# Two layers of a diffusion backbone on one core: one feed-forward input product by Strassen's scheme, and the adaLN modulations on TensorE

## The chip, the core and the metric

The kernel runs on one core of one Trainium2 chip, in one launch. The metric is the device time of that core in microseconds. Five engines run side by side, each through its own list of instructions, in the order in which they stand there: TensorE (PE in the profile; its weight loads are PEld), VectorE (DVE), ScalarE (ACT), GpSimd (POOL) and SyncE (SP), which here issues most DMAs. They wait for each other with semaphores.

## The reference

512 latent tokens and 256 context tokens of 1024 numbers, all float32. Each of two layers is a half-step SwiGLU feed-forward network (FFN), a mixer of four head groups, and a second FFN. Cut to what the change touches:

```
ml = ada_mods(silu(c), w_ada[l], b_ada[l])      # 9 * 1024 numbers for the latent tokens,
mc = ada_mods(silu(c_ctx), w_ada[l], b_ada[l])  # and as many for the context tokens
y = modulate(rms_norm(h, g), shift, scale)
a, b = split(y @ w_i, 2, axis=-1)               # w_i [1024, 5632]
h = h + 0.5 * gate * ((silu(a) * b) @ w_o)      # w_o [2816, 1024]
```

FFN 1 and FFN 2 of layer 0 and FFN 1 of layer 1 are needed for all 768 tokens, FFN 2 of layer 1 for the 512 latent ones alone.

## The kernel before

Everything lies transposed: features on the 128 partitions, tokens along the row. The residual is eight tiles `h[j]` of [128, 768]. `hg_tile` makes the input of a product from each (the residual times gain and scale, the shift in two columns ahead of the tokens, so that a product has 770 columns), split in two float32r parts, high and low. The RMS factor `R` of a token is multiplied in behind the product.

`wload` brings 1 MB of weights (8 row blocks, 256 columns) to a `wraw` buffer of three; `wsplit` makes the high part `wh` on ACT (L378) and the low part `wl` on DVE (L379), of 128 columns at a time, in two buffers each. `mm` (L389) then multiplies three times for each row block: high by low, low by high, high by high. A product of 770 columns goes to two PSUM banks, as 258 columns and 512, so a column tile of 1024 rows takes 48 matmuls on PE.

`ffn` walks over 22 column tiles `f` of the hidden layer. Each takes two products (`a` and `b`, 96 matmuls), is multiplied by `R`, gets silu and product on ACT and DVE (L448 to L455), and is split into `uh` and `ul` (L458 ACT, L459 POOL). After each group of `FF` = 5, 5, 4, 4, 4 tiles the output product of that group follows: eight tiles `po`, each added to `h[j]` by DVE (L495).

The modulations are 18 pieces of 512 columns a layer. The first four of layer 0 are multiplied on TensorE by `ada_first` (L215): float32, two columns of weights, written to PSUM partitions 0, 32, 64 and 96 in turn. The other 32 pieces are made by `ada_steps`, as `hooks` between the column tiles: 16 multiply-adds of [128, 512] on DVE (L254, L256), then four float32 matmuls by ones, to the four strips of 32 PSUM partitions (L263), a copy on ACT (L265) and two transposes on PE (L268).

What is written in the code is not the order on the engines: a scheduler reorders the list of each engine when the program is built, so matmuls of several products stand mixed. The engines then run those fixed lists.

The mixer (`Mixer.run`) multiplies 16 column tiles by `w_in`, with S5 and RG-LRU work between them, then attention, then `out_proj` (L1236), whose last steps call `hg_tile` for the next FFN. `park` and `unpark` keep the residual in DRAM meanwhile.

## Time and profile before

| | us |
|---|---|
| median of 3 runs | 2879.5 (2876.4 to 2881.92) |
| the profiled execution, first to last instruction | 2877.7 |

| stage of the profiled execution | us | PE busy | DVE busy |
|---|---|---|---|
| start, to 81.6 | 81.6 | 65.5 | 54.6 |
| rest of layer 0 FFN 1, to 655.7 | 574.1 | 568.3 | 405.5 |
| layer 0 mixer, to 1021.4 | 365.7 | 352.7 | 237.3 |
| layer 0 FFN 2, to 1595.8 | 574.4 | 574.1 | 308.3 |
| layer 1 FFN 1, to 2180.5 | 584.7 | 584.2 | 352.2 |
| layer 1 mixer, to 2484.7 | 304.2 | 289.1 | 207.4 |
| layer 1 FFN 2 and final norm, to the end | 393.0 | 385.2 | 177.0 |

The page gives for each engine its busy time and, for groups of instructions, how often they ran, their time together and the mean of one. Matmuls are pipelined: a row's mean is longer than the step from one matmul to the next, so steps are read from a run of many, or from starts. A float32 matmul stands in the trace as two records (34 matmuls at L357 are 68 records), a float32r one as one.

### The profile page before, as it was taken

To read this page: it belongs to the slowest core of one execution; us is meant where nothing else is said; L and a number is where in the kernel's file an instruction comes from. 1 tells how busy PE (TensorE), PEld (TensorE's weight loads), DVE (VectorE), ACT (ScalarE), POOL (GpSimd) and SP (SyncE) were. 2 spreads that over 40 slices of the span, in tenths; PEclk is the share of its full clock that TensorE was granted. 3 is DMA by queue.
4 is the path that set the end of the run, shared out by engine and by line. 5 is a ranking of instruction groups with operands and counts; after the bars stand their busy time and mean duration, and the time that the engine had idled before them with its cause. 6 is when DMAs were issued, how large, how long until landed. Compare 5 with 4: busy or idle time off the path is not lost.

```text
span 2877.7 us, 43478 instructions
## 1 busy us (share of the span) xinstructions
PE 2819.1 (98%) x17293; PEld 2437.7 (85%) x17293; DVE 1742.3 (61%) x3178; ACT 906.5 (32%) x1478; POOL 757.7 (26%) x957
## 2 busy tenths in 40 slices
PE   7999999999999999999999999999999999999998
PEld 4888888888877888888888888888888887899998
DVE  6868577676857566363634766465466876444445
ACT  4212121235546422112123321222224645322223
POOL 2822233221323311000001176332312434201001
PEclk9999999999999999999999999999999999999999
DMA  6445324353323333222311335233254343232231
GB/s 227 134 108 167 112 96 141 123 185 118 115 62 74 103 115 99 87 96 95 107 54 54 118 101 142 80 123 106 74 168 145 118 106 89 79 96 83 88 96 52
DMA packets 295901, 312.13 MB, mean 108 GB/s; under 512 B 58991, under 2 KB 243202, under 8 KB 295698
## 3 DMA queue, kind: packets, MB, share of 16 engines
q1 hardware_dynamic: 266990, 293.97, 31.8%
q0 software_dynamic: 5664, 12.59, 1.9%
q10 hardware_dynamic: 23044, 2.78, 0.7%
q8 instruction: 137, 2.24, 0.3%
q14 instruction: 66, 0.54, 0.1%
HBM read 276.09 MB, written 29.02 MB: 106 GB/s over the span
## 4 chain that ended last, share of the span: by engine, by line
PE 88%; DVE 6%; DMA 2%; ACT 2%; issue 1%; POOL 0%; SPq 0%; ACTq 0%; DVEq 0%; POOLq 0%
PE pi L389 51%; PE po L389 23%; PE po L1236 4%; DVE acc L256 2%; PE po L862 2%; PE pt L810 2%; DMA wa<-in_w_ada_dram 1%; PE ps L793 1%; PE pa L263 1%; DVE wl L379 1%; PE ps L794 1%; DMA l<-in_w_ada_dram 1%; PE pl L734 1%; DVE z L455 0%; PE pa L215 0%
## 5 line engine op out<-in xcount | busy, mean ns | idle before, releaser
L389 PE MATMUL pi<-g,wh 128*128 128x258 f32 (+2 forms) x6656 | 1408.7, 330 | 8.4 <-ACT wh L378 2.6
L389 PEld LDWEIGHTS pi<-g,wh 128*128 128x128 f32 x6656 | 1101.4, 191 | 132.2 <-issue 15.0
L389 PE MATMUL pi<-g,wl 128*128 128x258 f32 (+2 forms) x3328 | 828.1, 329 | 0.7 <-DVE wl L379 0.7
L378 ACT CAST wh<-wr 128x1024 fp32r<-128x1024 f32 (+3 forms) x380 | 338.2, 890 | 1397.4 <-PE pi L389 674.8
L389 PEld LDWEIGHTS pi<-g,wl 128*128 128x128 f32 x3328 | 607.4, 191 | 60.6 <-issue 2.5
L389 PE MATMUL po<-l,wh 128*128 128x512 f32 (+1 forms) x2464 | 566.1, 344 | 0.9 <-DVE e L495 0.8
L389 PEld LDWEIGHTS po<-l,wh 128*128 128x128 f32 x2464 | 387.9, 188 | 63.9 <-issue 3.9
L459 POOL TENSOR_TENSOR l<-z,l 128x768 fp32r<-128x768 f32 (+1 forms) x88 | 159.1, 1808 | 1061.4 <-ACT l L458 955.4
L379 DVE TENSOR_TENSOR wl<-wr,wh 128x1024 fp32r<-128x1024 f32 (+3 forms) x380 | 407.0, 1071 | 50.3 <-ACT wh L378 47.5
L256 DVE SCALAR_TENSOR_TENSOR acc<-wa,s,acc 128x512 f32<-128x512 f32 x448 | 358.6, 849 | 39.4 <-DMA wa<-in_w_ada_dram 38.6
L495 DVE SCALAR_TENSOR_TENSOR e<-po,gt,e 128x512 f32<-128x512 f32 (+1 forms) x296 | 176.2, 631 | 307.4 <-PE po L389 250.7
L389 PE MATMUL po<-l,wl 128*128 128x512 f32 (+1 forms) x1232 | 337.5, 343 | 1.0 <-DVE wl L379 1.0
L453 DVE TENSOR_TENSOR z<-pi,R 128x768 f32<-128x768 f32 (+2 forms) x91 | 78.4, 865 | 301.3 <-PE pi L389 301.3
L389 PEld LDWEIGHTS po<-l,wl 128*128 128x128 f32 x1232 | 194.5, 188 | 32.6 <-DVE wl L379 2.0
L448 DVE COPY bc<-pi 128x2 f32<-128x2 f32 x88 | 13.7, 156 | 189.4 <-PE pi L389 189.4
L458 ACT CAST l<-z 128x768 fp32r<-128x768 f32 (+1 forms) x88 | 68.8, 782 | 160.5 <-DVE z L455 160.5
L1545 POOL TENSOR_TENSOR ww<-AR,BB 128x256 f32<-128x256 f32 x32 | 25.9, 808 | 341.4 <-PE pw L1564 309.5
L455 DVE SCALAR_TENSOR_TENSOR z<-z,pi,z 128x512 f32<-128x512 f32 (+1 forms) x154 | 107.1, 730 | 5.5 <-ACT z L451 0.7
L317 POOL TENSOR_TENSOR ssq<-ssq,sq 128x768 f32<-128x768 f32 (+1 forms) x35 | 67.5, 1929 | 161.0 <-ACT sq L316 161.0
L451 ACT ACTIVATE z<-z,bc 128x512 f32<-128x512 f32 (+1 forms) x154 | 90.0, 625 | 62.7 <-DVE z L449 51.3
L449 DVE TENSOR_TENSOR z<-pi,R 128x768 f32<-128x768 f32 (+1 forms) x88 | 77.5, 880 | 3.7 <-ACT R L366 3.7
L1236 PE MATMUL po<-l,wh 128*128 128x512 f32 (+1 forms) x264 | 71.9, 356 | 0.0
(349 smaller groups left out, 2632.0 us busy)
## 6 DMA issues: line engine op xcount, KB each, us to landing
wr<-in_w_ffn_in_dram SPq DMA_DIRECT2D x88, 1024.0 KB
wa<-in_w_ada_dram SPq DMA_DIRECT2D x64, 1024.0 KB
wr<-in_w_ffn_out_dram SPq DMA_DIRECT2D x48, 512.0 KB
wr<-in_w_ffn_out_dram SPq DMA_DIRECT2D x32, 640.0 KB
wr<-in_w_in_dram SPq DMA_DIRECT2D x16, 1024.0 KB
W<-s5w SPq DMA_DIRECT2D x32, 256.0 KB
wr<-in_w_out_dram SPq DMA_DIRECT2D x8, 1024.0 KB
l<-in_w_ada_dram SPq DMA_DIRECT2D x24, 256.0 KB
```

The costliest lines, as they stand in the source:

```text
L256: nc.vector.scalar_tensor_tensor(acc[r], raw[:, k], s, acc[r], ALU.mult, ALU.add)
L378: nc.scalar.copy(hi[:, :kn], raw[:, :, o:o + P])
L379: nc.vector.tensor_sub(lo[:, :kn], raw[:, :, o:o + P], hi[:, :kn].bitcast(F32))
L389: nc.tensor.matmul(dst, lhsT=wt[:, k, :], rhs=xt[:, a:b], start=(k == 0 and i == 0), stop=(k == kn - 1 and i == 2))
L449: nc.vector.tensor_mul(ta[:, :nt], pa[:, 256:256 + nt], self.R[:, :nt])
L451: nc.scalar.activation(ta[:, a:b], ta[:, a:b], AF.Silu, bias=bc[:, i:i + 1])
L453: nc.vector.tensor_mul(tb[:, a:b], p, self.R[:, a:b])
L455: nc.vector.scalar_tensor_tensor(tb[:, a:b], tb[:, a:b], pb[:, 254 + i:255 + i], ta[:, a:b], ALU.add, ALU.mult)
L458: nc.scalar.copy(uh[:, :nt], tb[:, :nt])
L459: nc.gpsimd.tensor_sub(ul[:, :nt], tb[:, :nt], uh[:, :nt].bitcast(F32))
L495: self.nc.vector.scalar_tensor_tensor(self.h[j][:, a:b], ps[:, a:b], gate[:, j, i:i + 1], self.h[j][:, a:b], ALU.mult, ALU.add)
L1236: self.nc.tensor.matmul(dst, lhsT=wt[:, k, :], rhs=xt[:, a:b], start=(c == 0 and i == 0), stop=(c == NT - 1 and i == 2))
```

## The change

1. `STRASSEN` names layer 0's FFN 2. There the 2 by 2 blocks are: `a` and `b` columns of the weights, even and odd row blocks of 128, first and second 384 tokens. `st_tile` makes seven input combinations, each split in two parts, during `out_proj`. `st_weights` makes seven weight combinations from raw weights, four of them on POOL, and `two` splits them. `st_in` runs seven products of 4 row blocks and 384 or 386 columns (12 matmuls each), each to a PSUM tile of its own, and DVE adds them up in SBUF; the multiplication by `R` goes to POOL.
2. `ada_steps` multiplies on TensorE: eight float32 matmuls of 512 columns with 32 columns of weights, to the strips of 32 PSUM partitions in turn, and four small float32 matmuls by `sel` in place of the transposes. DVE keeps the bias alone.
3. Products of 770 columns are cut 386 and 384 instead of 258 and 512.
4. `wload` brings 128 columns (0.5 MB) of an input product at a time; `wraw` has five buffers of half the size.
5. `FF` is 4, 4, 4, 4, 3, 3. Tiles and pools move: the cosines and sines are loaded in the mixer to two `z` tiles, the low parts for `out_proj` lie in `g` and `e` tiles.

```diff
-SLOTS = {"e": 8, "l": 12, "z": 5, "g": 16}
+SLOTS = {"e": 8, "l": 12, "g": 16}
+Z_SLOTS, X_SLOTS = 5, 12
+W_BUFS = {"wh": 2, "wl": 2, "ws": 1}
-FF = (5, 5, 4, 4, 4)
+FF = (4, 4, 4, 4, 3, 3)
-        self.wraw = ent(tc.tile_pool(name="wraw", bufs=3))
+        self.wraw = ent(tc.tile_pool(name="wraw", bufs=5))
...
     def ada_steps(self, l, q):
...
         def rows(k0):
-            raw = (ring() if ring else self.wraw).tile([P, 4, 512], F32, name=self.nm("wa"), tag="wraw")
-            for k in range(4):
-                for r in range(2):
-                    s = self.s2[:, k0 + k, r:r + 1]
...
-                        nc.vector.scalar_tensor_tensor(acc[r], raw[:, k], s, acc[r], ALU.mult, ALU.add)
+            if k0 == 0:
+                st["ps"] = self.bank("pa", "pst")
+            for k in range(k0, k0 + 4):
+                if k % 2 == 0:
+                    raw = self.wraw.tile([P, 2, 512], F32, name=self.nm("wa"), tag="wraw")
+                    nc.sync.dma_start(raw, ...)
+                o = 32 * (k % 4)
+                nc.tensor.matmul(st["ps"][o:o + 32], lhsT=self.s2w[:, 2 * k:2 * k + 32], rhs=raw[:, k % 2], start=(k < 4), stop=(k >= 4))
         def done():
-            for i in range(4):
-                nc.tensor.matmul(ps[32 * i:32 * i + 32], lhsT=self.ones.to_broadcast([P, 32]), rhs=acc[i // 2]..., start=True, stop=True)
-            nc.scalar.copy(arow, ps)
-            for b in range(2):
-                nc.tensor.transpose(pt[:, b * P:(b + 1) * P], arow[:, b * P:(b + 1) * P], self.ident)
+            nc.scalar.copy(arow, st["ps"])
+            for b in range(4):
+                nc.tensor.matmul(pt[:, 2 * b:2 * b + 2], lhsT=arow[:, b * P:(b + 1) * P], rhs=self.sel, start=True, stop=True)
...
     def in_chunks(self, ps, nt):
-        return (ps[:, 254:512], (0, 258)), (ps[:, 512:256 + nt], (258, nt + 2))
+        o, m = self.at(nt), nt // 2 + 2
+        return (ps[:, o - 2:512], (0, m)), (ps[:, 512:o + nt], (m, nt + 2))
...
+    def st_weights(self, ra, rb):
+        (a11, a12), (a21, a22) = ((t[:, :4], t[:, 4:]) for t in (ra, rb))
+        s12 = self.wtile("ws", F32)
+        s2, s1 = s12[:, :4], s12[:, 4:]
+        yield from parts(ra)
+        G.tensor_add(s1, a21, a22)
+        G.tensor_sub(s2, s1, a11)
+        yield from parts(s12)
+        G.tensor_sub(a11, a11, a21)
+        G.tensor_sub(a12, a12, s2)
+        yield from parts(ra)
+        yield from parts(a22)
+    def st_in(self, ra, rb, nt):
+        def product(i, n):
+            dst = self.bank("pi") if i % 2 else self.psb.tile([P, 1024], F32, name=self.nm("pi"), tag="psb")
+            self.mm(((dst[:, :n], (0, n)),), next(ws), lambda k: self.sx[k][i], 4)
+            return dst[:, :n]
+        nc.scalar.copy(c21, product(0, w))
+        V.tensor_add(c11, product(1, w), c21)
+        V.tensor_add(c21, product(2, w), c21)
+        V.tensor_add(c12, product(3, m), c21[:, :m])
+        p = product(4, w)
+        V.tensor_add(c21, p, c21)
+        V.tensor_add(c22, p[:, :m], c12)
+        V.tensor_add(c12, product(5, m), c12)
+        nc.gpsimd.tensor_mul(a_, a_, R)
...
+        V.tensor_add(c21, product(6, w), c21)
+        nc.gpsimd.tensor_mul(b_, b_, R)
...
+STRASSEN = ((0, "ffn2"),)
```

How it moves instructions, at two places of layer 0's FFN 2. On PE before, a piece of modulation was one run of matmuls between two output tiles (`pa` is the PSUM strip, `po` an output tile, x2 two in a row to different strips):

```order
L389 MATMUL po_12341<-l_12186,wh_12337 128x512
L389 MATMUL po_12341<-l_12186,wh_12337 128x256
L263 MATMUL pa_12857<-acc_12713,ones 32x256 x2
L263 MATMUL pa_12857<-acc_12715,ones 32x256 x2
L389 MATMUL po_12372<-l_11486,wh_12368 128x512
L389 MATMUL po_12372<-l_11486,wh_12368 128x256
```

On PE of the changed kernel, in the second column tile of that FFN, between two of the seven products (L424 is `mm`, L282 a modulation product, L291 the small ones by `sel`):

```order
L424 MATMUL pi_10148<-x_9736,wh_10151 128x386
L424 MATMUL pi_10148<-x_9736,wl_10152 128x386
L424 MATMUL pi_10148<-x_9736,wh_10151 128x386
L282 MATMUL pa_10245<-wa_10396,s2w 32x512 x2
L291 MATMUL pt_10101<-sel,l_10099 128x2 x4
L424 MATMUL pi_10134<-g_9252,wh_10117 128x386
L424 MATMUL pi_10134<-g_9252,wl_10118 128x386
```

The eight products of a piece stand in several such runs, mostly of two. In the whole program the 256 products stand in 93 runs: 57 of two, 12 of one, 4 of three, 10 of four, 10 of six or eight; the 128 matmuls by ones stood in 44 runs.

On ACT before, in the same FFN, a column tile needs two weight parts (L378), and they stand among silu (L451) and the split (L458):

```order
L378 CAST wh_11092<-wr_11088 128x1024
L451 ACTIVATE z_11063<-z_11063,bc_11062 128x512
L451 ACTIVATE z_11063<-z_11063,bc_11062 128x256
L378 CAST wh_11145<-wr_11090 128x1024
L458 CAST l_11072<-z_11064 128x768
L378 CAST wh_11233<-wr_11088 128x1024
```

On ACT of the changed kernel (L410 is the weight part, `ws` sums made on POOL, L614 the first of the seven PSUM tiles, L288 a modulation's copy):

```order
L410 CAST wh_10117<-wr_10107 128x1024
L625 ACTIVATE l_9950<-l_9950 128x512
L625 ACTIVATE l_9950<-l_9950 128x256
L410 CAST wh_10151<-ws_10116 128x1024
L535 CAST l_10078<-l_9951 128x768
L288 COPY l_10099<-pa_10082 128x512
L614 COPY l_10114<-pi_10115 128x386
L410 CAST wh_10185<-wr_10107 128x1024
L410 CAST wh_10221<-wr_10110 128x512
L410 CAST wh_10264<-wr_10254 128x1024
```

A column tile now takes three and a half parts of this size from the same two buffers, and the fourth, `wh_10221`, serves the last product alone.

## Rows read from the trace of the kernel before

**Rows 1.** The page: span, engines' busy time, and the granted clock in 40 slices.
```profile
span 2877.7 us, 43478 instructions
PE 2819.1 (98%) x17293; PEld 2437.7 (85%) x17293; DVE 1742.3 (61%) x3178; ACT 906.5 (32%) x1478; POOL 757.7 (26%) x957
PEclk9999999999999999999999999999999999999999
```
**Rows 2.** Stretches of FFNs: length, busy us (instructions) by engine, granted clock, DMA.
```profile
81.60:480.00 398.40, 396.80 (x2293) 340.30 (x2293) 279.65 (x450) 85.29 (x126) 154.04 (x217) 1.00 0.39 120
480.00:520.00 40.00, 36.43 (x198) 29.34 (x197) 35.52 (x46) 8.41 (x16) 16.22 (x16) 0.91 0.51 172
520.00:655.70 135.70, 135.02 (x777) 115.18 (x776) 90.37 (x147) 41.66 (x76) 34.26 (x29) 1.00 0.50 161
1021.40:1595.80 574.40, 574.12 (x3284) 495.87 (x3284) 308.28 (x489) 135.93 (x194) 53.55 (x31) 1.00 0.28 90
1595.80:2180.50 584.70, 584.21 (x3390) 506.75 (x3389) 352.17 (x619) 143.24 (x227) 222.64 (x338) 1.00 0.38 118
```
**Rows 3.** Chain that ended last: start, length, what; runs of one kind of matmul.
```profile
1325.59 34.10 PE pi L389 x192
...
2555.91 27.82 PE po L389 x120
2583.73 57.89 PE pi L389 x480
```
**Rows 4.** Timeline of PE: start, length, count; a run of L215, two float32 products.
```profile
44.60 0.39 PE L389 MATMUL pi<-g,wh 128*128 128x512 f32 x1
44.92 1.03 PE L215 MATMUL pa<-l,s 128*2 128x512 f32 x4
45.88 0.50 PE L389 MATMUL pi<-g,wh 128*128 128x512 f32 x1
46.22 0.40 PE L389 MATMUL pi<-g,wl 128*128 128x512 f32 x1
```
**Rows 5.** Timeline of PE: ten float32 products in one run.
```profile
53.09 1.46 PE L215 MATMUL pa<-l,s 128*2 128x512 f32 x10
53.97 0.59 PE L215 MATMUL pa<-z,s 128*2 128x512 f32 x2
54.38 0.60 PE L215 MATMUL pa<-l,s 128*2 128x512 f32 x2
54.40 1.44 PE L215 MATMUL pa<-z,s 128*2 128x512 f32 x6
```
**Rows 6.** Timeline of PE: a run of L263, two float32 products of 256 columns.
```profile
1171.69 0.51 PE L389 MATMUL pi<-g,wh 128*128 128x258 f32 x2
1172.13 0.62 PE L263 MATMUL pa<-acc,ones 128*32 128x256 f32 x4
1172.69 0.62 PE L389 MATMUL pi<-g,wl 128*128 128x258 f32 x2
1173.14 0.63 PE L389 MATMUL pi<-g,wh 128*128 128x258 f32 x3
```
**Rows 7.** Groups by shape: count, busy us, mean ns, idle before and releaser.
```profile
L268 PE MATMUL pt<-ident,z 128*128 128x128 f32 x64 | 12.2, 272 | 0.0
L357 PE MATMUL pr<-ones,ssq 128*128 128x1 f32 x68 | 8.5, 251 | 0.0
L378 ACT CAST wh<-wr 128x1024 fp32r<-128x1024 f32 x224 | 235.3, 1050 | 896.9 <-PE pi L389 518.7 <-issue 187.8 <-PE po L389 115.1
L379 DVE TENSOR_TENSOR wl<-wr,wh 128x1024 fp32r<-128x1024 f32 x224 | 285.9, 1276 | 30.3 <-ACT wh L378 28.1
L459 POOL TENSOR_TENSOR l<-z,l 128x768 fp32r<-128x768 f32 x66 | 127.2, 1927 | 736.5 <-ACT l L458 672.4 <-issue 47.1 <-DMA wa<-in_w_ada_dram 16.9
L951 POOL TENSOR_TENSOR e<-e,cos 128x512 f32<-128x512 f32 x6 | 9.8, 1648 | 10.0 <-PE pr L948 10.0
```
**Rows 8.** Who PE waited for: total us, times, longest.
```profile
PE pa L263 <- DVE acc L256: 4.2, 4, 2.1
```

More of the change, by code (lines that the diff above doesn't have):

```diff
@@ L72, in setup @@
         self.cols = [c.tile([P, P], F32, name=f"cols{l}") for l in range(3)]
-        self.cos, self.sin = (c.tile([P, TL], F32, name=x) for x in ("cos", "sin"))
         self.perm = c.tile([P, P], F32, name="perm")
@@ L155, in load_vectors @@
         if l == 2:
-            self.s2 = self.const.tile([P, NT, 2], F32, name="s2")
+            self.s2w = self.const.tile([P, 2 * NT + 30], F32, name="s2w")
+            nc.vector.memset(self.s2w, 0.0)
+            self.s2 = self.s2w[:, :2 * NT].rearrange("p (k r) -> p k r", r=2)
             for i in range(2):
                 nc.scalar.activation(self.s2[:, :, i], self.cols[2][:, 8 * i:8 * i + 8], AF.Silu)
+            self.sel = self.const.tile([P, 2], F32, name="sel")
+            strips = self.ident.rearrange("p (g x) -> p g x", g=4)[:, :, 0:2]
+            nc.vector.tensor_add(self.sel, strips[:, 0], strips[:, 1])
+            for g in (2, 3):
+                nc.vector.tensor_add(self.sel, self.sel, strips[:, g])
     def col(self, l, name, i=0, n=1):
@@ L388, in mm @@
                 for dst, (a, b) in chunks:
-                    nc.tensor.matmul(dst, lhsT=wt[:, k, :], rhs=xt[:, a:b], start=(k == 0 and i == 0),
+                    nc.tensor.matmul(dst, lhsT=wt[k], rhs=xt[:, a:b], start=(k == 0 and i == 0),
                                      stop=(k == kn - 1 and i == 2))
@@ new lines, in st_weights, with parts @@
+    def st_weights(self, ra, rb):
+        G = self.nc.gpsimd
+        (a11, a12), (a21, a22) = ((t[:, :4], t[:, 4:]) for t in (ra, rb))
+        def parts(w):
+            hi, lo = self.two(w)
+            for i in range(0, len(hi), 4):
+                yield hi[i:i + 4], lo[i:i + 4]
+        s12 = self.wtile("ws", F32)
[8 more added lines that the diff above has]
+        yield from parts(a22)
@@ L945, in gqa_turn @@
         n, nc = self.n, self.nc
+        cos, sin = (self.t("z", w=TL) for _ in range(2))
+        nc.sync.dma_start(cos, self.A["k_cos"])
+        nc.sync.dma_start(sin, self.A["k_sin"])
         for src in self.gts:
@@ L1235, in out_proj @@
                     for dst, (a, b) in ch:
-                        self.nc.tensor.matmul(dst, lhsT=wt[:, k, :], rhs=xt[:, a:b], start=(c == 0 and i == 0),
+                        self.nc.tensor.matmul(dst, lhsT=wt[k], rhs=xt[:, a:b], start=(c == 0 and i == 0),
                                               stop=(c == NT - 1 and i == 2))
@@ L1632, in body @@
         hooks = [[] for _ in range(NFF)]
-        ring = []
         if not last:
-            spread(hooks, [s for q in range(ADA_2) for s in n.ada_steps(1, q, lambda: ring[0])])
+            spread(hooks, [s for q in range(ADA_2) for s in n.ada_steps(1, q)])
         end = None if last else lambda j: fin(j, 1, "ffn1", "g_ffn1", 0, TT)
-        with tc.tile_pool(name=n.nm("ring"), bufs=3 if last else 2, reuse_waits="tile") as more:
-            ring.append(more)
-            n.ffn(l, A["w_ffn2_in"][l], A["w_ffn2_out"][l], lambda: n.gate(l, 8, 0.5), nt, end, hooks, ring=more if last else None)
+        n.ffn(l, A["w_ffn2_in"][l], A["w_ffn2_out"][l], lambda: n.gate(l, 8, 0.5), nt, end, hooks)
+        n.room(0 if last else Z_SLOTS, 0)
         if not last:
```

234 lines of the change are left out of this document (155 added, 79 removed).

## The prediction

> **What bounds the kernel now.** I read the page first. PE is busy for 2819.1 of 2877.7 us [rows 1], but that alone says little, since matmuls overlap; so I looked next at the stretches of the FFNs [rows 2]. In layer 0's FFN 2 PE is busy for 574.12 of 574.40 us, in layer 1's FFN 1 for 584.21 of 584.70, at full clock. In the third, from 81.6 to 655.7, PE idles for 1.6 + 3.6 + 0.7 = 5.9 us, and only between 480 and 520 is the granted clock below full (0.91). Whether "busy" means "at its pace" is seen from runs in the chain [rows 3]: 192 matmuls of two column tiles took 34.10 us, a step of 0.1776 us; 480 of 256 or 258 columns took 57.89 us, 0.1206 each; 120 of 512 columns took 27.82 us, 0.2318 each. The two column tiles in the middle of a layer, with all its side work, run at the pace that the two sizes give together (0.1206 + 0.2318 = 0.352 a pair, against 0.355). So in the FFNs PE's list is the time. DVE is not behind it: PE waited for the modulations' sums on DVE for 4.2 us in all [rows 8], in 4 waits. From this I take the method: count what the change takes from PE's list and what it puts in, price both from rows, and then ask where PE would newly wait.
>
> **Strassen's products.** A column tile had 96 matmuls of 385 columns on average; seven products of 12 are 84. 22 tiles x 12 = 264 matmuls less, at 0.1776 us: **-46.9 us**, all of it on the path, as PE had no idle time there [rows 2, 3].
>
> **The modulations on TensorE.** Added are 256 float32 products of 512 columns, in 93 runs. Their price is read from the first modulations, which have that size and go to strips of 32 partitions [rows 4]. From 44.60 to 46.22 there are 1.62 us, in which two float32r matmuls of 512 columns would have taken 2 x 0.2318; so a run of two products (four records) costs 1.15 us. Where ten stand together [rows 5], a new set of records begins 0.43 us after the last one (53.97, 54.40); a product has two passes, so a round is 0.86 us, and up to four products to different strips share one. The remaining 0.29 us is the way in and out. That the number in a round doesn't matter is also seen from the old matmuls by ones [rows 6]: from 1171.69 to 1173.14 are 1.45 us, less four float32r matmuls (two of the pairs above, 0.71) is 0.74 for two products of 256 columns, and 0.74 is again one round of half the length (0.43) plus 0.31. So what counts is the number of runs and rounds, and not that of the products. 83 runs have one round and 10 have two (six or eight products over four strips): 83 x 1.15 + 10 x 2.01 = 115.6 us.
>
> The Trainium skill's page "TensorEngine Tiling (Array Packing)", section Overview / Key Properties, says that a change of the tiling mode drains the engine. The trace agrees: 0.3 us beyond the rounds at each run.
>
> Added too are 128 small products by `sel`, 256 records; nearest is L357, 8.5 us for 68 records [rows 7], 0.125 each: 32 us. Removed are 44 runs of matmuls by ones at 0.74 = 32.6 us, and 64 transposes, 12.2 us [rows 7]. Together 115.6 + 32 - 32.6 - 12.2 = **+102.8 us** on PE. Bounds: 103 rounds at 0.86 with nothing lost on the way in and out would be 27 us less; if the small products cost what a transpose does (0.19), 17 us more.
>
> **DVE is relieved** of 16 operations a piece. What PE can get from it is what PE lost to it: the 3.6 us of idle time between 480 and 520, and 40 x 0.09 = 3.6 us of slow clock there [rows 2]: **-7 us** (0 to -10, with the other 2.3 us of idle time in that FFN).
>
> **A new short distance on the weights' buffers.** Two `wh` and two `wl` buffers remain. Before, a buffer served 48 matmuls, 8.5 us, and the next split had that long. Now it serves two products, 24 matmuls or 4.26 us, and the one for the seventh product 12 matmuls, 2.13 us. The split for the next tile's first two products can start only when the fifth and sixth are done, and only the seventh covers it. ACT needs 1.05 us and DVE 1.28 behind it [rows 7], 2.33 us before any queueing, against 2.13. Since ACT and DVE run in order and have sums, silu and splits queued, I take 0.5 us a tile: 22 x 0.5 = **+11 us**. It can be nothing, where runs of modulations or output tiles stand between, and 2 us a tile (44) at worst, when a sum and a silu always stand ahead. POOL has four sums of 512 (1.65 each by L951), two multiplications of 768 (1.93 by L459, which is a subtraction) and one subtraction of 768 a tile: 12.4 us of the 14.9 that seven products take; it fits, with little to spare, and before the output tiles it has time to recover.
>
> **The start of that FFN.** The last residual tile `h[7]` gets its place in SBUF from the low part of `out_proj`'s last operand, so its load from DRAM starts only when `out_proj` ends, and then come the residual's addition, scaling, splits and the sum of squares. PE has the first three row block pairs of four products to go on with, 36 matmuls or 6.4 us. I take **+3 us** (0 to 8), and **+2 us** (0 to 10) for both mixers, where the same holds and two of five `z` tiles now hold cosines and sines while S5 uses the others.
>
> **The even cut.** 386 and 384 columns in place of 258 and 512 give the same number of matmuls and columns. If the step is proportional to columns it costs nothing: 0.2318 / 512 = 0.453 ns a column against 0.1206 / 257 = 0.469 for the short one. No row has 384 columns, so the bounds are these two: 770 columns at 0.453 is 0.349 a pair and at 0.469 is 0.361, against 0.355, so -6 to +6 ns; with some 5,400 pairs (24 a product tile of 768 tokens, 24 a row block of outputs, so 1584 an FFN in three FFNs, some 130 fewer with Strassen, and 800 in the mixers) that is -33 to +33 us. I take **0**, as the mean of the two is the step of the mixed run. The groups of `FF` change no count on PE, smaller loads are off the path (DMA share 0.28 to 0.39 in the long stretches [rows 2]), and the start is bound by the first modulations, which stay: 0.
>
> **The sum.** -46.9 + 102.8 - 7 + 11 + 3 + 2 = +64.9. From the profiled execution's 2877.7 that is 2942.6; it lay 1.8 us below the median of the runs, so I forecast **2944 us**, slower by 2.2%. The saved matmuls are worth less than half of what the modulations add to the one engine that had no room, while DVE, which did them beside, had.
>
> **The rivals.**
>
> *Products packed four at a time.* 256 products over four strips are 64 rounds at least, 55 us in place of 115.6 if the way in and out were free: 2944 - 61 = 2883, no change. It would need PE to fill strips across the matmuls that stand between; its list is fixed, 69 of the 93 runs hold one or two products, and the runs of the old kernel paid for each stop [rows 6]. Chance 0.05.
>
> The Trainium skill's "TensorEngine Tiling (Array Packing)", Overview / Theoretical Speedup, gives up to four times for products of 32 columns or less; by that rule the rounds would be those 64. No row here shows strips shared across other matmuls.
>
> *The strips run beside the main stream.* A modulation product uses a quarter or a half of the array's columns. If the matmuls around it went on meanwhile, the 115.6 us would vanish: 2944 - 116 = 2828, faster by 1.8%. The place is each of the 93 runs, the price 0 to 1.15 us, and it turns the sign where a run costs less than about 0.45 us. Against it: between 44.92 and 45.88 no float32r matmul started [rows 4], nor between 1172.13 and 1172.69 [rows 6]. Chance 0.05.
>
> *The weights' split becomes the bound of Strassen's stage.* At 2 us a tile PE stands for 44 us rather than 11: 2977; with POOL late as well (12.4 of 14.9 us), another 1 us a tile: 3000. For it: three chained engines and 0.2 us too little cover before any queue. Against: ACT and DVE have time (ACT's stage total was 136 of 574 us, DVE's 308 with the modulations in it [rows 2]). Chance 0.13.
>
> *Strassen's saving doesn't come*, since a product of half the depth pays for its start: nothing in the steps shows a price for a new PSUM tile. It would be 2991. Chance 0.03.
>
> **How the numbers follow.** The forecast, with the even cut at either bound, has 0.73 (2905 to 2985); the others as given, 0.01 left. Slower by over 0.2% (about what a measurement of this kernel can tell from no change): 0.73 + 0.13 + 0.03 = 0.89; same: 0.05; faster: 0.06. The range takes in the low bound of the products and of the even cut (together, -40 rather than their sum of -60, as they are independent) and on the other side the split's bound: 2904 to 2990.
>
> **What would show it.** In the profile after, L282 should have 512 records, and PE's main stream a gap of 1.1 to 1.2 us at each of its runs, also where two products stand alone. The seven products should run at 0.177 us a matmul, so that layer 0's FFN 2 has 22 x 14.9 + 187 us of L424, and with nine pieces of modulation (3.2 each) ends some 4 us below its 574. Layer 1's FFN 1 should be longer by about 9 x 3.2 = 29 us and layer 0's by more, though DVE is nearly free there. A wait of PE for `wl` once in a tile shows the buffers. I am wrong at the root if the FFNs without Strassen don't grow, wrong in size if the L282 gaps are not 1.15 us, and if the output tiles change their step from 0.355 a pair, it is the even cut.

## The result, and the profile after

The changed kernel takes **3021.4 us** (median of 4 runs, 3019.0 to 3022.7) against 2878.3 (4 runs) before: a ratio of **1.0498, 95% interval 1.0483 to 1.0513**. Slower was right; 5.0% instead of the 2.2% forecast was not, and 3021 lies 31 us outside the range of 2904 to 2990. The profiled execution has 3020.2 us against 2877.7, so +142.5 us are to be explained where +64.9 were forecast.

First the page of the changed kernel: PE has 89.6 us more busy time than in [rows 1], so 53 us of the 142.5 are PE standing still.

```profile
span 3020.2 us, 44606 instructions
PE 2908.7 (96%) x17453; PEld 2673.8 (89%) x17453; DVE 1553.1 (51%) x2897; ACT 974.4 (32%) x1602; POOL 919.6 (30%) x1117
```

Then the changed kernel by stretches: FFN 1 of layer 0, its mixer, its FFN 2 (Strassen's stage), layer 1's FFN 1, mixer and FFN 2. The columns are those of [rows 2].

```profile
81.60:679.00 597.40, 595.80 (x3446) 557.46 (x3445) 249.20 (x533) 139.74 (x226) 199.14 (x334) 1.00 0.44 128
679.00:1047.90 368.90, 356.51 (x2337) 327.78 (x2336) 244.29 (x498) 194.81 (x356) 126.20 (x138) 0.97 0.31 86
1047.90:1698.60 650.70, 599.88 (x3145) 543.87 (x3144) 363.48 (x508) 184.85 (x275) 244.35 (x160) 0.96 0.28 84
1698.60:2314.30 615.70, 613.81 (x3516) 583.42 (x3515) 261.07 (x499) 147.34 (x235) 207.92 (x337) 1.00 0.38 111
2314.30:2622.60 308.30, 287.65 (x1933) 254.74 (x1932) 206.48 (x419) 157.49 (x270) 96.04 (x106) 0.98 0.37 100
2622.60:3020.20 397.60, 387.00 (x2773) 364.62 (x2771) 184.54 (x300) 117.36 (x185) 42.93 (x36) 0.99 0.29 86
```

Layer 1's FFN 1 is read at once: 615.7 against 584.7 in [rows 2], +31 where 29 were forecast, with PE busy for 613.81 of its time. That is partly luck: r3 (below) shows 6.6 of the 31 to come from the rest of the change, so that the modulations cost 24 here. The miss is the third row. There PE was to be busy throughout and to end 4 us below 574.4; it took 650.7, stands still for 50.8 of them, and the granted clock is 0.96 (1.00 before): nine stretches of 3.4 to 6.8 us, 51.2 us in all, are at the 1.2 GHz level. Who PE waited for there (columns as in [rows 8]: total us, times, longest):

```profile
PE pt L291 <- ACT l L288: 26.5, 8, 5.0
PE pi L424 <- DVE wl L411: 9.7, 10, 1.1
PE pi L424 <- ACT l L614: 5.6, 5, 1.3
```

L291 are the small products by `sel`; L288 is ACT's copy of the piece that they read. In layer 1's FFN 1 there is no such wait. One of the eight as it stands in the timeline of the changed kernel (start, length; all engines, 1223 to 1238):

```profile
1226.44 2.12 DVE L411 TENSOR_TENSOR wl<-ws,wh 128x1024 fp32r<-128x1024 f32 x1
...
1227.44 2.26 POOL L598 TENSOR_TENSOR wr<-wr,ws 128x512 f32<-128x512 f32 x1
1229.66 1.55 POOL L627 TENSOR_TENSOR l<-l,R 128x768 f32<-128x768 f32 x1
...
1231.24 3.13 DVE L629 SCALAR_TENSOR_TENSOR l<-l,l 128x512 f32<-128x512 f32 x2 [2.68 <-POOL l L627]
...
1234.46 0.83 ACT L535 CAST l<-l 128x768 fp32r<-128x768 f32 x1 [7.44 <-DVE l L629]
1235.20 0.58 ACT L288 COPY l<-pa 128x512 f32<-128x512 f32 x1
1235.68 0.49 ACT L614 COPY l<-pi 128x386 f32<-128x386 f32 x1
...
1235.83 1.87 PE L291 MATMUL pt<-sel,l 128*128 128x2 f32 x8 [5.02 <-ACT l L288]
```

Read from the bottom up: PE stands 5.02 us for the copy. The copy needs 0.58 us and its `pa` had been ready since the last modulation product at 1217.4, but ACT runs in order and the `u` split of the column tile before (L535) is ahead of it, 7.44 us idle for DVE's L629. That waits for POOL's multiplication L627, behind POOL's L598, which takes 2.26 us beside the split of the weights on DVE and 1.28 without it. What the clock then does shows in two stretches of 6.8 us, the wait and what follows it (1.00, then 0.50):

```profile
1228.50:1235.30 6.80, 2.20 (x11) 1.88 (x11) 3.20 (x3) 0.84 (x2) 5.52 (x4) 1.00 0.00 0
1235.30:1242.10 6.80, 6.27 (x22) 6.27 (x23) 0.39 (x2) 1.10 (x3) 1.55 (x1) 0.50 0.01 2
```

### The profile page after: what moved, and what is told of

It is laid out like the page before. It is cut to its first block, busy times and chain, and to the rows that moved or that the text cites. A ratio compares the mean times of both kernels' runs of the same rounds, so it can differ in the third digit from the quotient of the medians.

```text
span 3020.2 us, 44606 instructions
## 1 busy us (share of the span) xinstructions
PE 2908.7 (96%) x17453; PEld 2673.8 (89%) x17453; DVE 1553.1 (51%) x2897; ACT 974.4 (32%) x1602; POOL 919.6 (30%) x1117
## 3 DMA queue, kind: packets, MB, share of 16 engines
q8 instruction: 138, 2.26, 0.3%
## 5 line engine op out<-in xcount | busy, mean ns | idle before, releaser
L424 PE MATMUL pi<-g,wh 128*128 128x386 f32 (+2 forms) x5952 | 1314.6, 330 | 10.0 <-ACT l L614 5.6
L424 PEld LDWEIGHTS pi<-g,wh 128*128 128x128 f32 x5952 | 1019.5, 192 | 63.5 <-issue 28.1
L410 ACT CAST wh<-wr 128x1024 fp32r<-128x1024 f32 (+2 forms) x434 | 358.3, 826 | 1404.7 <-PE pi L424 674.4
L424 PE MATMUL pi<-g,wl 128*128 128x384 f32 (+3 forms) x2976 | 773.3, 330 | 12.0 <-DVE wl L411 11.1
L424 PE MATMUL po<-l,wh 128*128 128x384 f32 (+2 forms) x2464 | 576.2, 345 | 6.4 <-DVE dt L358 2.8
L424 PEld LDWEIGHTS pi<-g,wl 128*128 128x128 f32 x2976 | 531.1, 192 | 30.8 <-DVE wl L411 23.3
L424 PEld LDWEIGHTS po<-l,wh 128*128 128x128 f32 x2464 | 439.2, 188 | 45.6 <-ACT wh L410 20.1
L411 DVE TENSOR_TENSOR wl<-wr,wh 128x1024 fp32r<-128x1024 f32 (+2 forms) x434 | 458.1, 1056 | 36.6 <-ACT wh L410 31.9
L635 DVE SCALAR_TENSOR_TENSOR e<-po,gt,e 128x512 f32<-128x512 f32 x352 | 209.5, 631 | 336.5 <-PE po L424 306.8
L424 PE MATMUL po<-l,wl 128*128 128x384 f32 (+2 forms) x1232 | 339.6, 345 | 1.5 <-DVE wl L411 1.4
L424 PEld LDWEIGHTS po<-l,wl 128*128 128x128 f32 x1232 | 223.8, 188 | 16.8 <-DVE wl L411 7.2
L424 PE MATMUL pi<-x,wh 128*128 128x386 f32 (+1 forms) x528 | 166.0, 348 | 1.4 <-DVE x L565 1.4
L282 PE MATMUL pa<-wa,s2w 128*32 128x512 f32 x512 | 106.6, 603 | 3.5 <-DMA wa<-in_w_ada_dram 3.5
L424 PEld LDWEIGHTS pi<-x,wh 128*128 128x128 f32 x528 | 102.3, 196 | 1.7 <-DVE x L565 1.7
L424 PE MATMUL pi<-x,wl 128*128 128x386 f32 (+1 forms) x264 | 91.6, 347 | 0.0
L623 POOL TENSOR_TENSOR l<-l,R 128x768 f32<-128x768 f32 x22 | 34.7, 1577 | 180.7 <-DVE l L621 176.3
L597 POOL TENSOR_TENSOR wr<-wr,wr 128x512 f32<-128x512 f32 x22 | 28.5, 1293 | 148.5 <-DVE wl L411 105.0
```

The costliest lines, as they stand in the source:

```text
L282: nc.tensor.matmul(st["ps"][o:o + 32], lhsT=self.s2w[:, 2 * k:2 * k + 32], rhs=raw[:, k % 2], start=(k < 4), stop=(k >= 4))
L410: nc.scalar.copy(hi, src)
L411: nc.vector.tensor_sub(lo, src, hi.bitcast(F32))
L424: nc.tensor.matmul(dst, lhsT=wt[k], rhs=xt[:, a:b], start=(k == 0 and i == 0), stop=(k == kn - 1 and i == 2))
L623: nc.gpsimd.tensor_mul(a_, a_, R)
L635: self.nc.vector.scalar_tensor_tensor(self.h[j][:, a:b], ps[:, o + a:o + b], gate[:, j, i:i + 1], self.h[j][:, a:b], ALU.mult, ALU.add)
```

## The experiments

The runs were made in five sets, each with the kernel before beside it: 2880.1 us beside the runs e, 2878.4 beside p, 2879.7 beside q, 2880.6 beside r, 2878.9 beside x and v. The ratio is to that. "Stage" is layer 0's FFN 2 in the profiled execution, from one sum of squares on PE to the next, 574.3 us before and 650.5 in the changed kernel. e6 and p1 to p4 leave nine pieces of modulation out, so that their totals are to be compared with each other alone. Each edit also lets the scheduler order the lists anew: a run shows what the edit is worth with the order that comes with it.

| run | edit | total us | ratio, 95% | stage us |
|---|---|---|---|---|
| e1_no_strassen | changed kernel, no Strassen | 2976.8 | 1.0323–1.0354 | 604.1 |
| e2_strassen_dve | Strassen, modulations on VectorE | 2941.4 | 1.0199–1.0230 | 625.3 |
| e3_late_turn | L291 later | 2973.5 | 1.0305–1.0340 | 602.2 |
| r3_neither | neither edit | 2901.0 | 1.0052–1.0082 | 576.5 |
| e6_no_mods_in_stage | no modulations in the stage | 2935.5 | 1.0180–1.0211 | 565.5 |
| p1_psum_halves | e6, six PSUM banks | 2986.7 | 1.0361–1.0392 | 612.2 |
| p2_seventh_buffers | e6, own buffers for product 7 | 2901.8 | 1.0067–1.0097 | 529.2 |
| p3_both | e6, p1 and p2 | 2931.7 | 1.0175–1.0205 | 560.7 |
| p4_scale_on_dve | e6, L623, L627 on DVE | 2927.7 | 1.0152–1.0186 | 557.6 |
| q2_seventh_only | changed kernel, own buffers | 2983.2 | 1.0346–1.0377 | 611.5 |
| q1_late_turn_seventh | own buffers, L291 later | 2952.1 | 1.0236–1.0266 | 576.0 |
| x1_copy_on_dve | changed kernel, L288 on DVE | 3011.3 | 1.0439–1.0474 | 637.7 |
| x2_scale_on_dve | changed kernel, L623, L627 on DVE | 2997.6 | 1.0396–1.0427 | 619.9 |
| q3_dve_seventh | e2, own buffers | 2923.4 | 1.0140–1.0170 | 605.5 |
| q4_dve_seventh_six | q3, 6 pieces in the stage | 2895.5 | 1.0036–1.0070 | 570.1 |
| r1_dve_four | q3, 4 pieces | 2889.8 | 1.0016–1.0039 | 561.4 |
| r2_dve_none | q3, 0 pieces | 2886.3 | 1.0005–1.0026 | 532.0 |
| v2_dve_mixer | r2, four pieces in the mixer | 2896.8 | 1.0043–1.0073 | 533.7 |

**The two edits apart.** e1 takes Strassen back, e2 the modulations, r3 both:

```
-STRASSEN = ((0, "ffn2"),)
+STRASSEN = ()
```

> The changed kernel with Strassen's algorithm taken back in layer 0's FFN 2 (96 matmuls a column tile as before); the modulations stay on TensorE. The changed kernel took 3021 us, and its layer 0 FFN 2 took 650.7 us where 570 were forecast, with PE standing 26.5 us at the small products by sel (L291) for ACT's copy and about 34 us in short gaps between main matmuls. Theory A (the two edits meet: copies of modulations stand in ACT's row among Strassen's weight parts, PE waits for them and the clock falls afterwards) and theory B (Strassen's own chain of weight parts and buffers makes the stalls) both give here 574.4 + 29 = 603 us for that FFN and about 2973 us for the kernel. Theory C (the modulations' runs cost more in this stage than the 3.2 us a piece seen in layer 1's FFN 1) gives a stage above 625 and 2995 us or more.

2976.8, stage 604.1: as theories A and B said, and C is out. Per edit, with r3: the rest of the change costs 2901.0 - 2880.6 = 20.4 us, the modulations on TensorE 2976.8 - 2901.0 = 75.8, Strassen on top 3021.4 - 2976.8 = 44.6, where the prediction has -46.9 + 11 + 3.

> Strassen's algorithm alone: the changed kernel with the modulations back on VectorE (16 operations a piece, then four matmuls by ones), loaded in tiles of two row blocks. Theory A (the stalls need both edits): layer 0's FFN 2 comes out at the forecast for Strassen alone, 574.4 - 46.9 + 11 + 3 = 541.5 us, and the kernel at about 2850 us, faster than before by 1%. Theory B (Strassen's own chain of weight parts makes the stalls): the stage keeps the short gaps and most of the slow clock, 575 to 600 us, and the kernel is at 2880 to 2905, no faster than before. Either way layer 1's FFN 1 goes back from 615.7 to about 585.

2941 is above what either theory said: Strassen with the modulations still on VectorE is slower than before. Its stage is 625.3 against 576.5 without it (r3), with PE waiting 26.7 us for `wl` in 22 places. So theory A, that only the two edits together stall, is out.

**L291 later.** The small products go into a list that the next step of modulations empties:

```
-            pt = self.bank("pt")[:, :8]
+            self.todo.append(lambda: turn(arow))
+        def turn(arow):
+            pt = self.bank("pt")[:, :8]
...
         def rows(k0):
+            self.flush()
```

> The changed kernel, with one edit: the four small products by sel (L291) of a piece are issued with the next step of modulations instead of right behind ACT's copy, so that on PE 96 or more main matmuls lie between in most places. Theory A: the 26.5 us of waits at these products go, and with them most of the stretches at the 1.2 GHz level (some 22 us); layer 0's FFN 2 falls from 650.7 to about 602, and the kernel from 3021 to about 2972. Theory B: the waits move to the next thing that ACT or the weight buffers owe PE; the stage falls by less than 15 us, and the kernel is at 3005 or above.

2973.5 and 602.2: theory A's numbers. Yet e2 had shown B at work as well. Both causes exist; this one is worth 48 us. In the trace of this kernel the wait at the small products (now L300) is 4.0 us where it was 26.5, and the stretches at the 1.2 GHz level are 17.1 us where they were 51.2.

```profile
PE pi L433 <- ACT l L624: 7.6, 8, 1.8
PE pi L433 <- DVE wl L420: 7.2, 8, 1.1
PE pt L300 <- ACT l L294: 4.0, 2, 3.0
```

**Strassen's stage by itself.** The nine pieces that stood as hooks in that FFN are left out:

```
-            spread(hooks, [s for q in range(ADA_2) for s in n.ada_steps(1, q)])
+            n.nc.gpsimd.memset(n.mods[1][:, :4 * ADA_2, :], 0.0)
```

> The changed kernel without the nine pieces of modulation in layer 0's FFN 2 (they are left out; the first 36 columns of layer 1's modulations are set to zero), so that Strassen's stage has nothing beside it. Theory A: the stage takes 574.4 less 46.9 for Strassen's products, less about 10 for the old matmuls by ones and transposes, plus 11 for the weight buffers and 3 for the start, 531 us, and the kernel 3021 - 120 = 2901. Theory B: the gaps and the slow clock stay without the modulations; the stage takes 570 us or more and the kernel 2940 or more.

565.5, between the two and near theory B's 570: with nothing beside it, Strassen's stage is 34 us above the 531 of its terms. Who PE waited for in it:

```profile
PE pi L424 <- ACT l L614: 16.2, 10, 4.3
PE pi L424 <- DVE wl L411: 13.1, 15, 0.9
```

L614 empties the bank of the first product, and stands on ACT behind the same L535. `wl` is DVE's part of the weights; in all 15 places PE waits for the split of a tile's first two products, the one that the prediction's cover is about. p1 and p2 take one resource's shortage away each, p3 both, p4 (its edit is that of x2, below) a link of the chain:

```
-            dst = self.bank("pi") if i % 2 else self.psb.tile([P, 1024], F32, ...)
+            if i % 4 == 0:
+                both.append(self.psb.tile([P, 1024], F32, ...))
+            dst = self.bank("pi") if i % 2 else both[-1][:, i % 4 * 256:i % 4 * 256 + 512]
...
-        yield from parts(a22)
+        yield from parts(a22, ("vh", "vl"))
...
-W_BUFS = {"wh": 2, "wl": 2, "ws": 1}
+W_BUFS = {"wh": 2, "wl": 2, "ws": 1, "vh": 1, "vl": 1}
```

> Strassen's stage by itself (layer 0's FFN 2 without its nine pieces of modulation, which are left out as in the run before it: 565.4 us for the stage, 2935 us in all, with 45.6 us of gaps between main matmuls at full clock), with one edit: products 0 and 2, and products 4 and 6, share a PSUM buffer of two banks, so that six banks rotate instead of four and product 4 no longer needs the bank that product 0 left. Theory P (ten to seventeen gaps of 1.5 us are product 4 waiting for the copy of product 0, L614, that stands on ACT behind the last tile's L535, which waits for DVE's L629): the waits for L614 (16.2 us) go; the stage falls by 16 to 20 us, to about 547, and the kernel to about 2917. Theory Q (DVE is late in any case, and PE stands at the next wl instead): the stage falls by less than 6 us.

A miss on both sides: the stage grew by 46.7 us. The waits for L614 are gone, as meant, but PE then ran ahead to the next `wl` and stood there once in each of the 22 tiles, longer than before, and the clock fell with it (0.96):

```profile
PE pi L424 <- DVE wl L411: 47.1, 22, 3.5
PE pi L424 <- DVE l L622: 8.2, 11, 0.8
```

> Strassen's stage by itself, as above, with one edit: the weight parts of the seventh product get buffers of their own (half size, one for each part), so that the two wh and two wl buffers serve six products in three pairs, and the split for the next tile's first pair can start one product earlier. Theory P (the short cover on the buffers, the term of 0.5 us a tile in the prediction): the waits for wl (13.1 us in 15 places, 0.9 each) go, the stage falls by 12 to 16 us, to about 551, and the kernel to about 2921. Theory Q (the split is late because DVE's subtraction takes 2.1 us beside POOL's work instead of 1.2, and not because its buffer is): the waits stay above 8 us, and the stage falls by less than 6.

529.2, more than theory P hoped for, and with own buffers nearly all waits went, those for L614 too:

```profile
PE pi L424 <- ACT l L614: 3.1, 1, 3.1
...
PE pi L424 <- DVE wl L411: 0.9, 1, 0.9
```

How the buffers act on both waits is seen in one column tile of e6 and one of p2 (start, length; rows of DVE, POOL and ACT together):

```profile
1107.32 1.55 POOL L623 TENSOR_TENSOR l<-l,R 128x768 f32<-128x768 f32 x1 [3.98 <-DVE l L621]
1107.76 2.19 DVE L411 TENSOR_TENSOR wl<-wr,wh 128x1024 fp32r<-128x1024 f32 x1 [0.52 <-DMA wr<-in_w_ffn_out_dram]
1109.87 0.55 DVE L626 TENSOR_TENSOR l<-pi,l 128x386 f32<-128x386 f32 x1
...
1113.58 1.54 POOL L627 TENSOR_TENSOR l<-l,R 128x768 f32<-128x768 f32 x1
...
1118.44 0.83 ACT L535 CAST l<-l 128x768 fp32r<-128x768 f32 x1 [3.13 <-DVE l L629]
```

```profile
1103.98 0.55 DVE L626 TENSOR_TENSOR l<-pi,l 128x386 f32<-128x386 f32 x1
1105.45 2.00 POOL L627 TENSOR_TENSOR l<-l,R 128x768 f32<-128x768 f32 x1
1109.73 0.84 ACT L535 CAST l<-l 128x768 fp32r<-128x768 f32 x1 [1.86 <-DVE l L629]
...
1112.78 1.22 DVE L411 TENSOR_TENSOR wl<-wr,wh 128x1024 fp32r<-128x1024 f32 x1
...
1116.64 1.55 POOL L623 TENSOR_TENSOR l<-l,R 128x768 f32<-128x768 f32 x1
```

In e6 the split of the first two products starts behind POOL's L623 and takes 2.18 us on average in 15 of 21 tiles; with own buffers it starts ahead of it and takes 1.22 in all 21. In the rows above L627 then begins 1.5 us behind the tile's last sum (L626) instead of 3.7, and L535 5.8 behind it instead of 8.6, so that L614 comes sooner too. The shared buffers are the cause here, and L614 is a place where it shows. 529.2 is 574.4 - 46.9 - 10 for the removed runs, and 12 more: PE stands still for 10.4 us. Strassen's saving exists.

> Strassen's stage by itself, as above, with both edits: shared PSUM buffers and own buffers for the seventh product's weights. If the two waits are separate, their gains add: the stage falls by about 30 us to 535, close to the 531 that the prediction's own terms give, and the kernel to about 2905. If both are one late chain on DVE, the stage stays above 550.

560.7, a miss for both. The gains do not add; shared PSUM tiles bring back 21.6 us of waits for the copy of the first product, 14 times. Why the program's order with shared tiles is worse stays open.

> Strassen's stage by itself, as above, with one edit: the two multiplications by R of a tile (L623 and L627, 44 operations of 1.6 us on POOL) move to DVE. In the run before, L411 took 2.15 us where L623 had begun ahead of it (14 times) and 1.22 us with POOL idle. Theory P (POOL's operations on SBUF hold up DVE's splits and sums of two SBUF operands, and PE waits for those): the splits of 1024 columns come down from a mean of 1.6 to 1.9 us towards 1.3, the waits for wl and L614 shrink by half or more, and the stage falls by 10 to 20 us although DVE has 44 more operations. Theory Q (the buffers set the waits): DVE has about 44 x 0.9 = 40 us more work, and the stage stays or grows by up to 10 us.

557.6, 8 us less, below what P expected; `wl` waits rose to 18.2 us in 32 places while those for L614 fell to 1.2. The first split is back at 1.22 us here too, in all 21 tiles, but 13.4 of the 18.2 us are now for the third split of a tile, with more work ahead of it on DVE. So p4 does not tell how much of the shared buffers' cost is the split's encounter with L623, and how much the short cover.

**Which link makes L288 late.** q2 frees the buffers, x1 and x2 move one operation each; q1 has both cures.

> The changed kernel with one edit: own buffers for the weight parts of the seventh product; the small products by sel (L291) stay right behind ACT's copy. Theory A1 (the copies L288 are late because ACT stands at weight casts whose buffers are not free, so that the buffers are the one cause of both waits): the stage falls from 650.7 to 575 or less, the waits at L291 from 26.5 us to below 10, and the kernel to about 2940. Theory A2 (PE reaches L291 some 4 us behind its last product, and ACT, in order, has casts ahead of the copy that wait for matmuls behind L291 whatever the buffers are): the waits at L291 stay above 18 us, the stage at 600 to 620, and the kernel at 2975 to 2990.

611.5, waits at L291 17.0 us in 8 places: close to A2, just below its 18. Buffers alone take 9.5 us from the wait at L291 and do not cure it.

> The changed kernel, all of its work in it, with two edits: the small products by sel (L291) are issued with the next step of modulations, and the weight parts of the seventh product have buffers of their own. The late small products alone brought layer 0's FFN 2 from 650.7 to 602.2 us; the own buffers brought Strassen's stage without modulations from 565.4 to 529.2. Theory A (two separate causes, PE waiting at L291 and the buffers): the gains add, the stage falls to 529 + 9 x 3.2 = 558 and a little for the waits left at L291, some 560 to 570, and the kernel to 2930 to 2940, the forecast's 2944. Theory B (with the modulations' runs between the products the buffers had their cover already, so the second edit is worth little): the stage stays above 590 and the kernel above 2960.

576.0 and 2952: between the two, nearer to A. The gains in the stage nearly add: 48.3 and 39.0 apart, 74.5 together.

```
-            nc.scalar.copy(arow, st["ps"])
+            nc.vector.tensor_copy(arow, st["ps"])
```

> The changed kernel with the copy L288 of a piece on DVE instead of ACT. In the changed kernel it stands on ACT right behind L535, the split of the column tile before, which waits for DVE's L629 (up to 7 us) and that for POOL's L627; PE stood 26.5 us at L291 for it, in 8 pieces. On DVE the program's order puts the copy right behind L629 itself, so that only L535's 0.83 us and a semaphore drop out. Theory L (the column tile's chain POOL L627, DVE L629 is what is late, whichever engine copies): the waits at L291 stay at 18 to 26 us, and the kernel at 3005 to 3020. Theory ACT (ACT's row is the cause): they fall below 10 us, and the kernel to about 2975.

The waits stay: 23.3 us, 8 times. 3011.3, between 3005 and 3020: theory L. The stage's 12.8 us less are mostly the clock: 27.3 us at the 1.2 GHz level instead of 51.2.

```profile
PE pt L291 <- DVE l L288: 23.3, 8, 4.2
```

```
-        nc.gpsimd.tensor_mul(a_, a_, R)
+        V.tensor_mul(a_, a_, R)
...
-        nc.gpsimd.tensor_mul(b_, b_, R)
+        V.tensor_mul(b_, b_, R)
```

> The changed kernel with the two multiplications by R (L623, L627) on DVE instead of POOL. In Strassen's stage without modulations this took 8 us off the stage. Theory L: POOL's row (L598 of 2.3 us, then L627, beside DVE's splits of 2.1) is the link that makes L629, L535 and the copy L288 late; with L627 on DVE the copy comes some 2 to 4 us sooner, the waits at L291 fall from 26.5 us to below 12 and layer 0's FFN 2 from 650.7 to 605 to 625, the kernel to 2975 to 2995. Theory DVE (DVE's own list is what is late): DVE has 40 us more work in the stage, the waits stay above 20, and the kernel above 3010.

The wait at L291 falls from 26.5 to 2.6 us and the stage to 619.9, both as theory L said, while `wl` takes up 20.6 us. The total, 2997.6, is 3 us above its span: layer 1's mixer takes 315 us here and 307 in the changed kernel.

```profile
PE pi L424 <- DVE wl L411: 20.6, 23, 2.1
...
PE pt L291 <- ACT l L288: 2.6, 5, 1.3
```

So it is the column tile's own chain over POOL and DVE that makes the copy late, and not the engine that copies.

**Can the saving be kept?** Strassen with own buffers, the modulations back on VectorE, and fewer and fewer of their pieces in the stage:

> Strassen's algorithm with the modulations on VectorE (2941 us, layer 0's FFN 2 at 625 us), with one edit: own buffers for the weight parts of the seventh product. Theory A (the short cover on the buffers is what turns DVE's queue into waits): the stage falls by the 36 us seen without modulations or more, to 545 to 590, and the kernel to 2865 to 2905. Theory D (DVE is simply too full, 480 us of work in the stage with VectorE's modulations in long runs ahead of the splits): the stage stays above 605, and the kernel above 2920.

> As the kernel before it in this set, with three of the nine pieces of modulation moved from layer 0's FFN 2 to layer 1's FFN 1 (six and twelve). Under theory A each piece costs Strassen's stage at least its 1.4 us on PE and some of its 11 us on DVE, and layer 1's FFN 1 only the 1.4: the kernel is 5 to 15 us faster than with nine, 2855 to 2890. Under theory D the stage gains 20 to 25 us from the three pieces, and the kernel stays above 2900.

> Strassen with own buffers for the seventh product and the modulations on VectorE, with four of layer 1's pieces in layer 0's FFN 2 and fourteen in layer 1's FFN 1 (nine and nine gave 605.5 us for the first and 591.2 for the second, six and twelve 570.1 and 598.2). If a piece on VectorE costs Strassen's stage the same each time, (605.5 - 570.1) / 3 = 11.8 us, the stage is at 547 and the next FFN at 603: 2877 in all, even with the kernel before. If only the pieces above some number do harm (a queue on DVE that is either full or not), the stage is at 535 to 540 or stays above 560.

> As above, with the first four pieces of layer 1's modulations in layer 0's FFN 1, so that Strassen's stage has none beside it. All of the computation is there. If Strassen's saving is real where nothing else is late, as in the run without modulations (529.2 us for the stage), then layer 0's FFN 1 takes 604 + 4 x 1.4 = 610 us, layer 1's 603, the mixers and layer 1's FFN 2 the 1041 to 1045 us of the kernel before it, and the kernel comes to 2845 to 2865, below the 2879 of the kernel before. If layer 0's FFN 1 gets too full on DVE (16 pieces of 11 us in 15 column tiles), it grows by 20 us or more and the kernel is at 2870 or above.

> Strassen with own buffers for the seventh product and all modulations on VectorE, the first four pieces of layer 1 in layer 0's mixer, where DVE has 120 of 365 us free, and the other fourteen in layer 1's FFN 1. With these four in layer 0's FFN 1 the stages took 631.2, 365.2, 532.0, 601.2, 306.2 and 370.3 us. If the mixer takes them for little more than their 1.4 us each on PE, it grows to 372 to 380, layer 0's FFN 1 falls back to 605, Strassen's stage stays at 532, and the kernel is at 2865 to 2875, below the 2880 of the kernel before. If DVE's chains in the mixer are as sensitive as Strassen's, it grows by 7 us a piece and the kernel is at 2885 or above.

q3 lies at the foot of theory D (605.5, 2923): DVE is busy for 465 of the 605 us, and PE waits for its sums. q4 misses both of its theories (35 us gained from three pieces, 2895). The stage takes 605.5, 570.1, 561.4 and 532.0 us with nine, six, four and no pieces; 11.8, 4.4 and 7.3 us a piece, so not in proportion, and the 547 expected of four was missed. Without any, Strassen's stage is at 532.0, 44 us below r3's; about 10 of these are the nine pieces that r3 has there and r2 has elsewhere. But the pieces cost wherever they go (the second branch of what was expected of r2 and v2): four in layer 0's FFN 1 make it 631.2 instead of 606.0, four in the mixer make it 401.7 instead of 365.2, the others in layer 1's FFN 1 601.2 instead of 591.4. The best, r2, is 2886.3 us, 0.15% above the kernel before. No version here beats it.

> The changed kernel with neither Strassen's algorithm nor the modulations on TensorE: what is left is the even cut of the column tiles, the new groups of FF, the smaller weight loads and the new places of buffers. The prediction takes all of it at +2 us, with the even cut between -33 and +33: layer 0's FFN 2 at 574 and the kernel at 2880 to 2885. Other runs with the modulations on VectorE showed 593 for layer 1's FFN 1 against 585 and 3 to 5 us more in each mixer; if that is the even cut or the loads and not DVE's fuller list, the kernel is at 2895 or above.

2901.0: the rest of the change is not free. The even cut is not what it costs: matmuls of 384 and 386 columns follow each other at 0.1761 and 0.1769 us on average in that kernel, and those of 512 with 256 or 258 at 0.2341 and 0.1196 before, 0.1768 a matmul. The 20 us are spread: 6.6 in layer 1's FFN 1, 10.0 in its mixer, 2 to 3 in each of three other stages. In that FFN 1 (591.40 us), PE now has 5.0 us idle where it had 0.5, 2.7 of them waiting for DVE's residual at the output tiles. Six groups instead of five make more of those. That is argued, not shown. In the mixer PE stands still 7 us more (two new waits of 5.6 and 5.4 us), and 23.9 us instead of 13.7 are at the 1.2 GHz level; which part of the change makes them stays open.

## Why the prediction was right or wrong, step by step

- **What bounds the kernel: right but for Strassen's stage.** PE's list is the time in the other FFNs; what was put into it came out as time. In the stage PE stands still for 50.8 us and runs 51.2 at the lower clock.
- **Modulations, +102.8: right, in mechanism and size.** L282 has its 512 records in 93 runs. A run costs the main stream 1.07 us with one product and 1.09 with four (1.15 forecast), 1.945 with two rounds (2.01); 83 x 1.07 + 10 x 1.945 = 108 us, against 115.6. In a row of the changed kernel's timeline, a run of two: 1.41 us from the pair of matmuls ahead to the pair behind, of which the pair takes 0.35.

```profile
1918.57 0.50 PE L424 MATMUL po<-l,wh 128*128 128x384 f32 x2
1919.00 1.05 PE L282 MATMUL pa<-wa,s2w 128*32 128x512 f32 x4
1919.98 0.62 PE L424 MATMUL po<-l,wh 128*128 128x384 f32 x2
```

  Two other terms were read from busy time, which is longer than the steps: the small products take 32 x 0.81 = 26 us, not 32, and what was removed took 34 (in r3 45 runs by ones of 0.66 us and 32 of transposes of 0.14), not 44.8. So 108 + 26 - 34 = 100. e1 agrees: with 80 runs its list grows by 68 x 1.073 + 12 x 1.945 + 26 - 34 = 88; against r3 PE stands still 8.3 us less and runs 8.9 less at the 1.2 GHz level, half of which counts; that makes 75, and 75.8 were measured. The Trainium skill's "TensorEngine Tiling (Array Packing)", Key Properties, puts the drain at each change of mode; the trace has 1.07 - 0.86 = 0.21 us for it. Both rivals that made these products cheap are out.
- **DVE's relief, -7: right.** In layer 0's FFN 1 PE stands still 4.4 us less in e1 than in r3 and runs 6.8 us less at the lower clock: 7.8.
- **Strassen's products, -46.9: right,** seen only in p2 and r2, where the stage is at 529 and 532. The seven products run at 0.177 us a matmul. The rival by which the saving does not come is out.
- **The weights' buffers, +11 (0.5 us a tile): the step that failed first.** They cost 36.3 us in the stage by itself (565.5 - 529.2), 39.0 in the changed kernel (650.5 - 611.5): 1.7 us a tile, close to the 2 us of the rival that I gave 0.13; its 2977 us lack the other cause, below. To set the cover of 2.13 us against the split of the next first pair was right, and PE waits for just that. Two things were wrong. DVE's part takes 2.18 us in most tiles, not 1.28, with POOL's L623 begun ahead of it; 1.05 + 2.18 - 2.13 is 1.1 us, and 0.9 a wait were measured, 13.1 us in all. And what stands behind the late split was put at nothing: POOL's L597, L598 and L627, DVE's L629, ACT's L535 and L614, which cost 16.2 us more of waits in e6. I had argued from totals that ACT and DVE have time; a total of busy time says nothing on that. Of the 36.3 us, 26.3 are PE standing still and 5 the lower clock; the last 5 are not traced.
- **What was missing: the wait at L291.** The 256 records were priced, but I did not ask what they wait for, though [rows 8] showed the old kernel's modulations waiting for another engine's sum. 48 us (e3): 27.6 of standing still (50.8 - 23.2), 22.5 of them at L291 (26.5 - 4.0), and of the stretches at the lower clock 34 us less (51.2 - 17.1), half of which, 17, is time lost; the last 3 are not traced.
- **POOL "fits, with little to spare": right as a sum, and no answer.** It is busy 244 of 650 us; the place of L623 and L627 in the chain made the splits and the copy late (p2, x2).
- **Start, mixers, rest, +5: too low.** r3 has 20.4 for all of it but Strassen's start. That lies inside the bounds given for the cut, but the cut costs nothing; layer 1's FFN 1 (6.6) and the two mixers (12.6), put at 0 and 2, hold most of it.

The sum by runs: 20.4 + 75.8 + 44.6 = 140.8, against 143.1 measured. The first two, 96.2, come near the forecast's 102.8 - 7 + 2 = 97.8 by luck: the rest cost 18 more than forecast and the modulations 20 less, 12 of these because e1 has 80 runs of them and not 93. The miss shows in Strassen's part: -33 forecast, +44.6 measured, among them the 12 us of the 13 further runs, which all stand in its stage (39 there, 26 in e1). In that stage: 604.1 us without it (e1), less 46.9, plus 74.5 for buffers and L291 together (650.5 - 576.0 in q1), plus 18.8 that q1 still has over that, which makes 650.5. Of the 74.5, 40 are standing still, 24 the lower clock and 7 the runs (39 against q1's 32); of the 18.8, 8.5 are standing still, 2 the clock and 6 the runs. The last 7 are not traced.

## What to carry to other kernels

Where PE's list is the time, price each new instruction on it twice: what it takes, and whom it waits for, following that engine's row back to what stands ahead of it. Put the consumer of another engine's copy a good stretch behind the producer; moving four small products later gave 48 us, at no cost that the runs show. When a buffer starts to serve fewer matmuls, compare its cover with the whole chain that refills it, with the durations that those operations have beside the new work, and expect a cure at another place to move the wait (p1, p3).

## What the runs showed of the hardware

- **DVE's two-operand operations and POOL's hold each other up.** In the changed kernel the split of 128x1024 (L411) takes 1.22 us where POOL is idle; where POOL's L623 had begun ahead of it, 2.18 us on average, 15 times of 15. Where the split had begun first, POOL's L598 took 2.27 us on average, 16 times of 16, and 1.28 otherwise. One of each stands in the rows of e6 above (L411 at 1107.76) and of the changed kernel (L598 at 1227.44).

  The Trainium skill's "SBUF — State Buffer", Who interferes with whom, says that a DVE instruction with two SBUF inputs and a GpSimd instruction that reads SBUF block each other, and that the one issued second waits. The trace agrees in both directions; it was the rule to weigh here, since the change puts 22 x 6 = 132 sums and products on POOL in that stage.
- **The clock falls behind a short stand-still.** After PE had stood 5.0 us it ran 6.8 us at the 1.2 GHz level though it was busy for 6.27 of them; before the change that FFN had no such stretch, after it nine, seven of which follow a wait of 3.0 to 5.0 us at L291. In p4 PE stands still for 26.3 us of the stage in waits of 1.9 us at most, and there is no such stretch.
- **A cure can move a wait and lengthen it.** p1 took away the 16.2 us for L614, and those for `wl` went from 13.1 to 47.1; with own buffers as well (p3) these are 4.4, but the copy's are back at 21.6.
